# Activations and the scaled input 48 bytes lower, and more products read in four passes, in a bidirectional encoder layer

## The chip, the cores and the metric

The kernel runs on one core of a Trainium2 chip. The metric is the device time of one execution in microseconds. Before the change the median of three runs is 835.85 us (835.64 to 836.09).

The core has a matrix engine (TensorE, with a separate instruction that loads the weights, "PEld" in the profile), VectorE (DVE), ScalarE (ACT), GpSimd (POOL) and SyncE (SP), which issues most transfers. A matrix product names a stationary operand of 128x128 ("weights") and a moving operand of 128 rows and up to 512 columns. Both lie in the on-chip memory, which has 128 partitions; an address in this document is a byte offset within a partition.

## The reference

The layer has a half-step feed-forward block, a mixer (Fourier groups beside attention), a second half-step block, and a last norm, on 512 positions of 1024 channels:

```
x = x + 1/2 * SwiGLU_1(RMSNorm(x))
h = RMSNorm(x); u = h @ w_in                 # [fourier 512 | q 512 | k 128 | v 128]
x = x + concat([A, B]) @ w_out               # A: Fourier mixer, B: attention
x = x + 1/2 * SwiGLU_2(RMSNorm(x))
y = RMSNorm_final(x)
def swiglu(h, w_gate, w_up, w_down):
    return (jax.nn.silu(h @ w_gate) * (h @ w_up)) @ w_down
```

The inner width of the feed-forward block is 2752, that is 21 chunks of 128 and a tail of 64. All is float32.

## The kernel before

**Split numbers.** Every float32 operand of a large product is split into a high and a low part, each in a rounded format that TensorE takes (`fp32r`). A product of weights W and moving operand M is then three matrix products that add up in one PSUM bank: W high with M high, W high with M low, W low with M high. The helper `product` issues them (lines 181, 183 and 184). ScalarE makes the high parts (a cast), VectorE the low ones (a subtraction, `lows`, line 123).

**Straight and turned.** `product` has an option `turn` (lines 176 to 180; the matrix product itself stands on line 179). `turned` (line 172) views 512 columns as 32 blocks of four granules of four numbers, and goes over the first granule of every block, then over the second of every block, and so on: four passes, each in pieces of 16 bytes that lie 64 bytes apart. Both the moving operand and the PSUM output are walked in that order, so that each number lands where it did before. Down products of the full 512 positions are turned; all others are read straight through.

**Feed-forward block (`ffn`, line 277).** The chunks are in four groups. In the first group (3 or 4 chunks with the tail, "plain"), gate and up are computed directly from the scaled input h: `gate` (line 303) loads the weights of one chunk, splits them into two slots, and issues 8 x 3 products of 128x512. In the very first opening (`opening1`, line 680) the first four column chunks are computed together while x arrives, by the matrix product on line 703. The other chunks take seven half-size products instead of eight (`seven`, with products of 128x256 on line 415, moving operand `rt`). After each group the down products of this group are issued for eight blocks of output channels (`down`, line 480; the tail's products are on lines 497 and 498), and the result is added to x (line 538).

**Mixer.** The projections to q, k and v (`project_ops`, line 812) use `product` with h as the moving operand. The Fourier projection has h as the stationary operand and the weights as the moving one (lines 1008 to 1010). Everything in the mixer stands in an order written out by hand (`ORDER`), for all engines; in the feed-forward blocks TensorE and SyncE follow program order and a planner places the rest.

**Closing.** In the last block the final three channel blocks are computed with 128x256 products for the first half of the positions and then by position, with the activations as weights and the down weights as the moving operand (line 529, 128x384).

**Where things lie.** `ring` is one tile with 12 slots of 4096 bytes. Its first eight slots hold h, high part in the first half of a slot and low part in the second (`hh`, `hl`); later the same slots hold weights. Slots 8 to 11 are always weight slots; slots 10 and 11 lie a further 256 bytes up (`ROOM`). `at` holds the activations in seven places of 4096 bytes (2048 of high and 2048 of low part); while the first group runs, the last four places are lent as weight slots. In the mixer `more` gives two more slots. `room` puts unused bytes between tiles. By the allocation of the built program, `ring` begins at byte 16512, `at` at 119232, `rt` at 148032 and `more` at 119168; modulo 256 that is 128, 192, 64 and 128. `FURTHER` (in numbers of four bytes) moves the Fourier weights up within a slot, `SKIP` the down weights of the last three blocks.

Of the kernel before, what the change touches and what calls it, by code (L numbers as in the profile page):

```python
# [7 lines left out]
F32R = mybir.dt.float32r  # L8
# [5 lines left out]
P = 128  # L14
S = 512
D = 1024
KD = D // P
# [4 lines left out]
HD = 64  # L22
EPS = 1e-6
WARM = 9
FURTHER = 48
FURTHER_IN = "f0", "f1", "f2", "f3"
ROOM = 64
NS = 12

GROUPS1 = ((0, "t", 1, 2), range(3, 9), range(9, 15), range(15, 21))  # L30
# [3 lines left out]
USES = "a11", "a12", "s1", "s2", "s4", "s3", "a22"  # L34
PIECES = (0, 2, 2, 0, 2, 1, 1)
KH = KD // 2
SKIP = 32
LAST = 3
CUT = 1, P // 2
HI_DVE = ("f0", "f1")  # L40
# [43 lines left out]
def encoder(ctx, tc, A, out):  # L84
# [1 line left out]
    cp = ctx.enter_context(tc.tile_pool(name="const", bufs=1))  # L86
    wp = ctx.enter_context(tc.tile_pool(name="weights", bufs=3))

    ring = cp.tile([P, NS * KD * P + 2 * ROOM], F32R, name="ring")
    taken = []  # L90

    def room(pool, n):
# [15 lines left out]
    gains = gx[:, : 4 * KD].rearrange("p (n k) -> p n k", k=KD)  # L108
    xt = gx[:, 4 * KD :].rearrange("p (k s) -> p k s", s=S)
    x = [xt[:, k, :] for k in range(KD)]  # L110
    hh = [ring[:, k * KD * P : k * KD * P + S] for k in range(KD)]
    hl = [ring[:, k * KD * P + S : (k + 1) * KD * P] for k in range(KD)]


    def in_order():
# [161 lines left out]
    def ffn(norm, after, wgu, wd, wdt, groups, opening, closing):  # L277
# [4 lines left out]
        n_ = norm.n  # L282
        n_plain = len(groups[0])
        with tc.tile_pool(name=f"act{n_}", bufs=1) as ap, tc.tile_pool(name=f"sums{n_}", bufs=2) as sp:
            room(ap, 256)
            at = ap.tile([P, PLACES, 2, S], F32R, name=f"at{n_}")
            room(ap, 128)
            rt = ap.tile([P, 7, 2, KH, HALF], F32R, name=f"rt{n_}")
            wt, raws = [], {}
            free, where = list(range(PLACES)), {}  # L290
# [12 lines left out]
            def gate(c, between={}, by_dma=False):  # L303
                whi, wlo = weights(wgu[c], f"gu{n_}_{c}", by_dma=by_dma)
                ps = bank(f"gu{n_}_{c}")
                for k in range(KD):
                    between.get(k, int)()
                    product(ps, whi[:, k, :], wlo[:, k, :], hh[k], hl[k], k == 0, k == KD - 1)
                return ps

            def tail_weights():
# [231 lines left out]
            for gi, group in enumerate(groups):  # L543
                last = gi == len(groups) - 1
                ahead = []
                if gi:
                    rest = seven(range(group[0] + 1, min(group[-1] + 2, NF)), ready)
                else:
                    lent = [at[:, i].rearrange("p a b -> p (a b)") for i in range(PLACES - 4, PLACES)]
                    plain.extend(lent)  # L550
                    row = []
                    pss = dict(enumerate(opening(gate, lambda: norm.column([norm.acc]), lambda: row.append(norm.row()))))
                    back(lent[:2])
                    due, parts, left = [*pss, "t"], list(range(KH)), range(2 * len(pss), 2 * n_plain)
                    pss["t"] = [gate(2 * NF)]
                    tail_weights()
                    for i, c in enumerate(left):
                        pss.setdefault(c // 2, []).append(gate(c, by_dma=i in (1,) if n_ else i > 0))
                        if due:
                            j = due.pop(0)  # L560
                            evacuate(at[:, place(j)], n_, pss[j], norm)
                        if c % 2 and c != left[-1]:
                            due.append(c // 2)
                        while len(parts) * len(left) > (len(left) - 1 - i) * KH:
                            o = parts.pop(0)
                            operands(row[0], o, o + 1)

                    def rest():
                        evacuate(at[:, place(n_plain - 1)], n_, pss[n_plain - 1], norm)

                def added(d, ps):
                    residual(d, ps, every)
                    if last:
                        (after.sums if closing else after.add)(d)
                    if ahead:
                        f, *a = ahead.pop(0)
                        f(*a)

                waiting, downs = [], []
                for d in range(KD):  # L580
                    if last and closing and d == KD - LAST:
                        closing(
                            [(e, down(e, group, gi)) for e in range(d, KD)], residual,
                            lambda ps, c: by_tokens(ps, c, group), finished,
                        )
                        break
                    if last and d == KD - 2:
                        back(lent)
                    ps = bank(f"dn{n_}_{d}_{gi}")
                    while len(downs) < min(d + 1 + (0 if gi or not n_ else 2), KD):  # L590
                        downs.append(down(len(downs), group, gi))
                    steps = downs[d](ps, every)
                    for _ in range(len(group) - (last and d < 2)):
                        next(steps)
                    waiting.append((d, ps, steps))
                    if d == (1 if gi or n_ else 2) and not last:
                        ready = prepare(groups[gi + 1][0] + 1)
                        ahead.extend(ready[1])
                    if d == 0:
                        rest()  # L600
                        if last:

                            lent = slots[KD - 2 : KD]
                            plain[2:2] = lent
                            continue
                    for d_, ps, steps in waiting:
                        for _ in steps:
                            pass
                        added(d_, ps)
                    waiting = []  # L610
                for f, *a in ahead:
                    f(*a)
                if not gi:
                    back(lent)
                free.extend(where[j] for j in group)
# [64 lines left out]
    def opening1(gate, column, row):  # L680

        pss = [bank(f"gu0_{c}") for c in range(4)]
        ws = []

        def highs(i, k):
            n0.scale_high(k, None if k else nc.vector)
            hi, _ = ws[i]
            for c in (slice(0, 2), slice(2, 4)) if k == 0 else (slice(0, 4),):
                nc.scalar.copy(hi[:, k % 2, c], raws[i][:, k % 2, c])

        def weight_lows(i, k):
            hi, lo = ws[i]
            lows(lo[:, k % 2], raws[i][:, k % 2], hi[:, k % 2])

        def products(k):
            hi, lo = ws[k // 2]
            passes = [(c, w, m) for w, m in ((hi, hh), (hi, hl), (lo, hh)) for c in range(4)]
            for n, (c, w, m) in enumerate(passes):
                if (k, n) == (6, 8):
                    sums()  # L700
                if (k, n) == (7, 4):
                    row()
                nc.tensor.matmul(  # L703
                    pss[c], w[:, k % 2, c], m[k], start=k == 0 and m is hh and w is hi,
                    stop=k == KD - 1 and w is lo,
                )

        ss = []

        def sums():  # L710
            ss.append(bank("ss0"))
            for c in range(4):
                n0.sum(ss[0], c, [n0.acc])

        with tc.manual_schedule(engines={mybir.EngineType.Activation, mybir.EngineType.DVE}):
            for k in range(KD):
                i = k // 2
                if k % 2 == 0:
                    ws.append(tuple(slot().rearrange("p (a c b) -> p a c b", a=2, b=P) for _ in range(2)))
                highs(i, k)  # L720
                if k < KD - 1:
                    n0.scale_low(k)
                    weight_lows(i, k)
                for j in {3: range(0, 4), 5: (4, 5), 6: (6, 7)}.get(k, ()):
                    n0.sums(j)
            for k in range(KD - 1):
                products(k)
            n0.scale_low(KD - 1)
            n0.mean(ss[0], 0, 4)
            n0.power(0, 4)  # L730
            weight_lows(KH - 1, KD - 1)
            products(KD - 1)
        nc.sync.dma_start(out=qkg, in_=A["qkg"])
        nc.sync.dma_start(out=fb, in_=A["fb"])
        return [pss[0:2], pss[2:4]]
# [6 lines left out]
    with tc.tile_pool(name="mix", bufs=1) as mp, tc.tile_pool(name="mixt", bufs=1) as mt:  # L742
# [69 lines left out]
        def project_ops(c, name):  # L812

            weight_ops(f"w{name}", A["wins"][c])

            def step(k):
                if k == 0:
                    banks[name] = bank_for(name, {"v": 1, "k": 3, "q0": 3}.get(name, 2))
                whi, wlo = ws[f"w{name}"]
                product(banks[name], whi[:, k, :], wlo[:, k, :], hh[k], hl[k], k == 0, k == KD - 1)  # L820

            for k in range(KD):
                op(f"{name}.{k}")(lambda k=k: step(k))
# [737 lines left out]
```

## Time and profile before

| what | time |
|---|---|
| median of three runs | 835.85 us |
| the profiled execution | 835.62 us |
| its span, first to last instruction | 833.8 us |
| TensorE busy in the span | 826.7 us, 5406 products |
| VectorE busy | 640.0 us |
| ScalarE busy | 465.1 us |
| granted TensorE clock, mean | 0.998 |

In the profile a group of instructions has its line, engine, operation, output and inputs, shape and count, then the busy time in us, the mean duration of one in ns, and the idle time just before. The durations of matrix products overlap, since a product starts while the one before it drains; how often a product can start is read from the starts in the timeline. In the timeline and in the chain the first number of a row is its start in us from the span's start, the second its length.

### The profile page before, as it was taken

To read this page: it belongs to the slowest core of one execution; us is meant where nothing else is said; L and a number is where in the kernel's file an instruction comes from. 1 tells how busy PE (TensorE), PEld (TensorE's weight loads), DVE (VectorE), ACT (ScalarE), POOL (GpSimd) and SP (SyncE) were. 2 spreads that over 40 slices of the span, in tenths; PEclk is the share of its full clock that TensorE was granted. 3 is DMA by queue.
4 is the path that set the end of the run, shared out by engine and by line. 5 is a ranking of instruction groups with operands and counts; after the bars stand their busy time and mean duration, and the time that the engine had idled before them with its cause. 6 is when DMAs were issued, how large, how long until landed. Compare 5 with 4: busy or idle time off the path is not lost.

```text
span 833.8 us, 13667 instructions
## 1 busy us (share of the span) xinstructions
PE 826.7 (99%) x5406; PEld 750.9 (90%) x5406; DVE 640.0 (77%) x1005; ACT 465.1 (56%) x778; POOL 30.7 (4%) x34
## 2 busy tenths in 40 slices
PE   9999999999999999999999999999999999999997
PEld 6888999899989998888998888899988999899986
DVE  7898896489756947699998488999955896479573
ACT  7773674157524645677786356656632674257462
POOL 0110000000000000221100000100000000000001
PEclk9999999999999999999999999999999999999999
DMA  7664322323242213522020224453232332322222
GB/s 253 170 144 167 129 93 77 121 102 139 74 141 98 65 55 114 177 94 79 26 76 26 73 88 130 109 170 121 89 116 88 133 116 66 135 102 95 68 75 102
DMA packets 31168, 89.58 MB, mean 107 GB/s; under 512 B 3712, under 2 KB 8832, under 8 KB 31104
## 3 DMA queue, kind: packets, MB, share of 16 engines
q1 hardware_dynamic: 27776, 82.61, 28.8%
q0 software_dynamic: 2608, 5.12, 3.3%
q10 hardware_dynamic: 720, 0.98, 0.3%
q8 instruction: 42, 0.69, 0.3%
q14 instruction: 22, 0.18, 0.1%
HBM read 84.24 MB, written 2.10 MB: 104 GB/s over the span
## 4 chain that ended last, share of the span: by engine, by line
PE 98%; issue 0%; DMA 0%; DVE 0%; ACT 0%; POOLq 0%; POOL 0%; DVEq 0%
PE dn L179 25%; PE r L415 23%; PE q L415 11%; PE p L415 6%; PE mix L181 3%; PE mix L184 3%; PE mix L183 3%; PE gu L703 3%; PE gu L181 3%; PE gu L183 3%; PE gu L184 3%; PE mix L1213 2%; PE mix L1170 2%; PE mix L1144 1%; PE mix L1008 1%; PE mix L1009 1%
## 5 line engine op out<-in xcount | busy, mean ns | idle before, releaser
L415 PE MATMUL r<-rt,ring 128*128 128x256 f32 x1686 | 209.5, 276 | 0.0
L179 PE MATMUL dn<-at,ring 128*128 128x512 f32 x900 | 205.4, 383 | 0.0
L415 PEld LDWEIGHTS r<-rt,ring 128*128 128x128 f32 x1686 | 200.5, 188 | 0.9
L179 PEld LDWEIGHTS dn<-at,ring 128*128 128x128 f32 x900 | 167.7, 187 | 31.5
L415 PE MATMUL q<-rt,ring 128*128 128x256 f32 x840 | 106.6, 276 | 0.0
L123 DVE TENSOR_TENSOR ring<-s,ring 128x1024 fp32r<-128x1024 f32 x70 | 85.4, 1220 | 24.1 <-ACT ring L374 20.8
L415 PEld LDWEIGHTS q<-rt,ring 128*128 128x128 f32 x840 | 100.4, 188 | 0.0
L538 DVE SCALAR_TENSOR_TENSOR gx<-dn,gx 128x512 f32<-128x512 f32 x61 | 41.9, 688 | 71.4 <-PE dn L179 71.3
L374 ACT CAST ring<-s 128x1024 fp32r<-128x1024 f32 x70 | 73.5, 1050 | 28.0 <-PE p L415 12.7
L165 ACT CAST ring<-raw_dn 128x768 fp32r<-128x768 f32 (+3 forms) x58 | 45.3, 784 | 75.4 <-PE dn L179 66.9
L123 DVE TENSOR_TENSOR ring<-raw_dn,ring 128x768 fp32r<-128x768 f32 (+3 forms) x58 | 51.5, 891 | 5.8 <-PE r L415 4.5
L415 PE MATMUL p<-rt,ring 128*128 128x256 f32 x420 | 53.3, 276 | 0.0
L123 DVE TENSOR_TENSOR ring<-raw_g,ring 128x1024 fp32r<-128x1024 f32 x35 | 42.6, 1218 | 10.3 <-PE p L415 10.3
L415 PEld LDWEIGHTS p<-rt,ring 128*128 128x128 f32 x420 | 50.2, 188 | 0.0
L374 ACT CAST ring<-raw_g 128x1024 fp32r<-128x1024 f32 x35 | 36.8, 1052 | 14.6 <-DMA raw_g<-in_wgu 8.8
L423 ACT COPY p<-r 128x256 f32<-128x256 f32 x35 | 13.0, 370 | 47.9 <-PE r L415 47.6
L447 ACT ACTIVATE g<-g 128x512 f32<-128x512 f32 x35 | 22.2, 633 | 23.4 <-DVE g L446 23.1
L383 ACT CAST ring<-raw_u 128x512 fp32r<-128x512 f32 x35 | 21.8, 624 | 16.5 <-PE q L415 15.9
L460 DVE TENSOR_TENSOR u<-g,u 128x512 f32<-128x512 f32 x35 | 24.0, 685 | 6.4 <-ACT u L459 6.4
L251 POOL TENSOR_TENSOR r<-ms,mhalf 128x4 f32<-128x4 f32 (+1 forms) x4 | 4.3, 1072 | 665.7 <-DVE ms L244 665.7
L181 PE MATMUL gu<-ring 128*128 128x512 f32 x72 | 28.2, 392 | 0.0
L123 DVE TENSOR_TENSOR at<-u,at 128x512 fp32r<-128x512 f32 x35 | 23.9, 684 | 5.5 <-ACT at L461 5.5
(310 smaller groups left out, 1471.0 us busy)
## 6 DMA issues: line engine op xcount, KB each, us to landing
raw_g<-in_wgu SPq DMA_DIRECT2D x35, 512.0 KB, 3.6
raw_u<-in_wgu SPq DMA_DIRECT2D x35, 512.0 KB, 4.3
raw_dn<-in_wd SPq DMA_DIRECT2D x40, 384.0 KB, 3.1
raw_gu<-in_wgu SPq DMA_DIRECT2D x12, 512.0 KB, 3.8
raw_o<-in_wo SPq DMA_DIRECT2D x8, 512.0 KB, 3.5
raw_dn<-in_wd SPq DMA_DIRECT2D x8, 448.0 KB, 3.3
raw_wq<-in_wins SPq DMA_DIRECT2D x4, 512.0 KB, 4.5
raw_f<-in_winf SPq DMA_DIRECT2D x4, 512.0 KB, 4.1
```

Of the source, the lines that this page charges most:

```text
L123: nc.vector.tensor_tensor(out=lo, in0=src, in1=asf(hi), op=ALU.subtract)
L165: nc.scalar.copy(hi[:, :n, :], raw[:, :n, :])
L179: nc.tensor.matmul(ps, a, b, start=first and b is mhi and a is whi, stop=last and a is wlo)
L181: nc.tensor.matmul(ps, whi, mhi, start=first, stop=False)
L183: nc.tensor.matmul(ps[:, t], whi, mlo[:, t], start=False, stop=False)
L184: nc.tensor.matmul(ps, wlo, mhi, start=False, stop=last)
L374: nc.scalar.copy(hi, src)
L415: nc.tensor.matmul(ps[:, t], a[:, ks], b[:, i, t], start=first and i == 0 and o == 0, stop=i == KH - 1 and o == 2, skip_group_check=not first,
L447: nc.scalar.activation(b["g"], b["g"], AF.Silu)
L460: nc.vector.tensor_tensor(out=u, in0=b["g"], in1=u, op=ALU.mult)
L538: nc.vector.scalar_tensor_tensor(out=x[d][:, t], in0=ps[:, t], scalar=0.5, in1=x[d][:, t], op0=ALU.mult, op1=ALU.add)
L703: nc.tensor.matmul(pss[c], w[:, k % 2, c], m[k], start=k == 0 and m is hh and w is hi, stop=k == KD - 1 and w is lo,)
```

## The change

The change alters where three things lie and how they are read; the operations and their order on each engine stay the same.

- The ring's tile begins with 16 numbers in front (`FRONT`), and the slots come after them, so that the slots and every tile allocated behind the ring lie 64 bytes higher. h starts 4 numbers from the tile's start (`NEAR`), which is 48 bytes below its slots and 16 bytes above where it was.
- The activations' tile gets 64 numbers more, in place of the 256 bytes of room before it, and the places start 16 - 12 = 4 numbers from its start (`LOWER`). The lent places stay 16 numbers from the start. The built program has the places at 119184, 48 bytes below 119232, and the lent ones at their old addresses; modulo 256 the ring's slots, `more`, the tail weights and the lent places are now at 192, h and the places at 144, `rt` at 128.
- `FURTHER` and `SKIP` become smaller by 12 and 28 numbers.
- Plain gate and up products, those of `opening1`, and the mixer's projections are turned.

A slot now reaches 48 bytes into the part of h that follows, and a lent place 48 bytes into the next place.

```diff
-FURTHER = 48
+FURTHER = 36
...
+FRONT, LOWER, NEAR = 16, -12, 4
...
-SKIP = 32
+SKIP = 4
...
-    ring = cp.tile([P, NS * KD * P + 2 * ROOM], F32R, name="ring")
+    whole = cp.tile([P, FRONT + NS * KD * P + 2 * ROOM], F32R, name="ring")
+    ring = whole[:, FRONT:]
...
-    hh = [ring[:, k * KD * P : k * KD * P + S] for k in range(KD)]
-    hl = [ring[:, k * KD * P + S : (k + 1) * KD * P] for k in range(KD)]
+    hh, hl = (
+        [whole[:, k * KD * P + o * S + NEAR : k * KD * P + (o + 1) * S + NEAR] for k in range(KD)] for o in range(2)
+    )
...
-            room(ap, 256)
-            at = ap.tile([P, PLACES, 2, S], F32R, name=f"at{n_}")
             room(ap, 128)
+            acts = ap.tile([P, PLACES * 2 * S + ROOM], F32R, name=f"at{n_}")
+            at = acts[:, FRONT + LOWER : FRONT + LOWER + PLACES * 2 * S].rearrange("p (n a b) -> p n a b", a=2, b=S)
...
-                    product(ps, whi[:, k, :], wlo[:, k, :], hh[k], hl[k], k == 0, k == KD - 1)
+                    product(ps, whi[:, k, :], wlo[:, k, :], hh[k], hl[k], k == 0, k == KD - 1, turn=True)
...
-                    lent = [at[:, i].rearrange("p a b -> p (a b)") for i in range(PLACES - 4, PLACES)]
+                    lent = [acts[:, FRONT + i * KD * P : FRONT + (i + 1) * KD * P] for i in range(PLACES - 4, PLACES)]
...
-                    pss[c], w[:, k % 2, c], m[k], start=k == 0 and m is hh and w is hi,
+                    turned(pss[c]), w[:, k % 2, c], turned(m[k]), start=k == 0 and m is hh and w is hi,
...
-                product(banks[name], whi[:, k, :], wlo[:, k, :], hh[k], hl[k], k == 0, k == KD - 1)
+                product(banks[name], whi[:, k, :], wlo[:, k, :], hh[k], hl[k], k == 0, k == KD - 1, turn=True)
```

## The prediction

> **What bounds the kernel now.** I read the page's totals first, then the chain that ended last, then the groups by form, and last the timeline, because only the distance from one start to the next tells what a matrix product costs here.
>
> ```profile
> span 833.8 us, 13667 instructions
> ...
> PE 826.7 (99%) x5406; PEld 750.9 (90%) x5406; DVE 640.0 (77%) x1005; ACT 465.1 (56%) x778; POOL 30.7 (4%) x34
> ...
> PE 98%; issue 0%; DMA 0%; DVE 0%; ACT 0%; POOLq 0%; POOL 0%; DVEq 0%
> PE dn L179 25%; PE r L415 23%; PE q L415 11%; PE p L415 6%; PE mix L181 3%; PE mix L184 3%; PE mix L183 3%; PE gu L703 3%; PE gu L181 3%; PE gu L183 3%; PE gu L184 3%; PE mix L1213 2%; PE mix L1170 2%; PE mix L1144 1%; PE mix L1008 1%; PE mix L1009 1%
> ```
>
> TensorE is the whole chain. Next, the groups that the change touches (count behind the x; lines 183 and 184 have a row like each of line 181, line 498 one like line 497), and one it leaves alone:
>
> ```profile
> L415 PE MATMUL r<-rt,ring 128*128 128x256 f32 x1674 | 209.3, 276 | 0.0
> L179 PE MATMUL dn<-at,ring 128*128 128x512 f32 x900 | 205.4, 383 | 0.0
> ...
> L181 PE MATMUL gu<-ring 128*128 128x512 f32 x72 | 28.2, 392 | 0.0
> ...
> L181 PE MATMUL mix<-ring 128*128 128x512 f32 x32 | 12.8, 400 | 0.0
> ...
> L179 PE MATMUL dn<-at 128*128 128x512 f32 x45 | 12.1, 387 | 0.0
> L703 PE MATMUL gu<-ring,at 128*128 128x512 f32 x48 | 11.9, 399 | 0.0
> L703 PE MATMUL gu<-ring 128*128 128x512 f32 x48 | 11.2, 392 | 0.3 <-ACT ring L689 0.3
> L181 PE MATMUL gu<-ring,at 128*128 128x512 f32 x24 | 9.5, 396 | 0.0
> ...
> L529 PE MATMUL last<-ring,at 128*128 128x384 f32 x42 | 8.5, 345 | 0.0
> ...
> L181 PE MATMUL mix<-ring,more 128*128 128x512 f32 x16 | 6.5, 408 | 0.0
> ...
> L497 PE MATMUL dn<-at,wt 128*128 128x512 f32 x16 | 6.2, 385 | 0.0
> ```
>
> They hardly wait (last column). Their durations overlap the next product, so the price is the distance of starts. From the timeline, plain gate products and mixer projections, all read straight through:
>
> ```profile
> 34.23 0.39 PE L181 MATMUL gu<-ring 128*128 128x512 f32 x1
> ...
> 39.67 0.40 PE L181 MATMUL gu<-ring,at 128*128 128x512 f32 x1
> ...
> 45.27 0.39 PE L181 MATMUL gu<-ring 128*128 128x512 f32 x1
> ```
>
> ```profile
> 336.02 0.39 PE L181 MATMUL mix<-ring 128*128 128x512 f32 x1
> ...
> 341.46 0.39 PE L181 MATMUL mix<-ring 128*128 128x512 f32 x1
> ```
>
> 24 products lie between each two rows: 5.44 us / 24 = 226.7 ns with weights in the ring, 5.60 / 24 = 233.3 ns with weights in a lent place of `at`, and 5.44 / 24 = 226.7 ns in the mixer. Down products already read in 4 passes; from the chain, and from the timeline of the first group:
>
> ```profile
> 137.39 28.13 PE dn L179 x126
> ```
>
> ```profile
> 59.34 0.38 PE L497 MATMUL dn<-at,wt 128*128 128x512 f32 x1
> 59.55 0.38 PE L498 MATMUL dn<-at,wt 128*128 128x512 f32 x1
> 59.77 2.14 PE L179 MATMUL dn<-at,ring 128*128 128x512 f32 x9
> 61.76 0.38 PE L497 MATMUL dn<-at,wt 128*128 128x512 f32 x1
> 61.98 0.38 PE L498 MATMUL dn<-at,wt 128*128 128x512 f32 x1
> 62.20 1.49 PE L179 MATMUL dn<-at,ring 128*128 128x512 f32 x6
> ...
> 72.09 1.52 PE L179 MATMUL dn<-at 128*128 128x512 f32 x6
> 73.45 0.83 PE L179 MATMUL dn<-at,ring 128*128 128x512 f32 x3
> ```
>
> 28.13 / 126 = 223.3 ns is the usual price. From 59.34 to 62.20 13 products take 2.86 us: 220.0 ns. From 72.09 to 73.45 6 products with weights in lent places take 226.7 ns. So the same shape costs 220 to 233 ns by pass order and by where the operands lie.
>
> **What the addresses do.** Call d the distance from the moving operand to the weights that are loaded during it, in bytes of a partition modulo 256. By the tiles' places before, d is 0 for gate and projections with weights in ring or `more`, 64 for gate weights in lent places, 192 for down with ring or tail weights, 0 for down with lent weights, 64 for the 128x256 products of line 415. So: straight through, d=0 gives 226.7 and d=64 gives 233.3; in 4 passes, d=192 gives 223.3 or 220.0 and d=0 gives 226.7. After the change ring, `more`, tail weights and lent places agree modulo 256 and h and the activations lie below them, so that d is 48 for every gate, up, projection and down product, lent or not. Those of line 415, and the 128x256 ones that `FURTHER` and `SKIP` are for, keep d=64, so their time stays. No row has d=48, nor any 128x512 read in 4 passes from a start that is not a multiple of 64 bytes: X, the price of a 4-pass product at d=48, is the unknown.
>
> **The change part by part.** On every engine the sequence of operations stays the same; no wait, DMA or instruction is added. X is bounded from below by a step as large as that between the two 4-pass prices under the lower one (220.0 - 3.3 = 216.7, an estimate, since no mean in the rows is less), and from above by the dearest place seen, 233.3. I take 220.0: it is the price that today's 4-pass products hold for a stretch, and d is now one value throughout, so nothing knocks them from it as the lent weights after 63 us do. No row proves this.
>
> The Trainium skill, "TensorE: Matmul & The Clock Gate", section "Step-by-step: what each phase is for", says that the weight load and the moving operand have read ports of their own, so the next load takes nothing from the running product. Then place would not matter, X would be today's 223.3, and the first rival below would come true; the 226.7 against 233.3 above, where only the weights' place differs, disagrees.
>
> With X = 220.0:
> - Gate and up, ring weights: 3 x 72 + 48 = 264 products x 6.7 = 1.77 us.
> - Gate and up, lent weights: 3 x 24 + 48 = 120 x 13.3 = 1.60 us, since these also leave d=64.
> - Projections: 3 x (32 + 16) = 144 x 6.7 = 0.96 us.
> - Down, ring weights: 900 x 3.3 = 2.97 us; lent: 45 x 6.7 = 0.30; tail: 2 x 16 = 32 x 3.3 = 0.11.
>
> Sum 7.7 us, all on the chain. Taken back:
>
> ```profile
> 28.70:56.20 27.50, 27.50 (x123) 22.59 (x122) 26.55 (x48) 21.97 (x31) 5.44 (x5) 1.00 0.75 159
> 536.40:551.00 14.60, 14.60 (x68) 12.11 (x66) 14.54 (x25) 6.51 (x11) 0.00 (x0) 1.00 0.50 164
> ```
>
> ```profile
> 24.42 2.11 PE L703 MATMUL gu<-ring,at 128*128 128x512 f32 x8
> 26.42 0.65 PE L256 MATMUL rp<-ident,r 128*128 128x128 f32 x4
> ```
>
> ```profile
> 24.84 1.53 POOL L251 TENSOR_TENSOR r<-ms,mhalf 128x4 f32<-128x4 f32 x1 [23.53 <-DVE ms L244]
> ```
>
> (Windows: stretch, its length, busy time of PE, weight loads, DVE, ACT, POOL.) In 28.70 to 56.20 TensorE would save 96 x 6.7 + 24 x 13.3 = 0.96 us, which leaves 26.54 against VectorE's 26.55: the cover is used up, and part of VectorE's idle time is its own waiting, so I take off 0.3. In 536.40 to 551.00 VectorE is busy for 14.54 of 14.60; of some 64 products' 0.37 us saved (14.45 / 64 = 225.8 each now) I count 0.3 as lost to its results coming no earlier. The norm's power ends at 24.84 + 1.53 = 26.37, the transposes start at 26.42: the 8 products between run 0.1 us shorter and wait for it. The closing's 42 products of 128x384 take their weights from `at` and move the ring, so they go from d=64 to d=208; by the step from 226.7 to 233.3 up to 42 x 6.7 = 0.28 us either way, and I take 0.2 lost. A ring slot now reaches 48 bytes into the next part of h, and a lent place 48 bytes into the next place; these new conflicts are between uses a whole stage apart: nothing, and if a cast had to wait, one 128x1024 cast's time, about 1 us. Writes by ACT and DVE at the new starts: nothing, as both are off the chain; a dearer write would show in the two windows above.
>
> In all 7.7 - 0.9 = 6.8 us off. The profiled execution took 835.62 us (span 833.8 and 1.8 around it), 0.23 under the median of 835.85: 835.62 - 6.8 = 828.8 us.
>
> **Rivals.**
> *The place does not matter (X = 223.3).* Order of passes alone counts. Gains 264 x 3.4 + 120 x 10.0 + 144 x 3.4 + 45 x 3.4 = 2.7 us, less 0.2 of cover: 833.1. For it: 126 products in a row at just this price. Against: 220.0 and 226.7 at other places.
> *A better place than any seen (X = 216.7).* 264 x 10.0 + 120 x 16.7 + 144 x 10.0 + 900 x 6.6 + 45 x 10.0 + 32 x 6.6 = 12.7 us, less about 1.4 of cover: 824.3. For it: 16-byte offsets were never tried in the rows, and 64-byte steps move the price by 6.7. Against: nothing has been that fast.
> *The weight load now collides with the passes (X = 226.7), slower.* d=48 lies between 0 and 64, and 4 passes at d=0 already cost 226.7. Lent gate products still gain 120 x 6.7 = 0.8, but down loses 900 x 3.4 + 32 x 3.4 = 3.2, and the closing 0.2: 838.2. It decides from X = 224.8 on, where the gate's gains and the down's losses cancel. At the worst place, 233.3, ring gate and projections lose 408 x 6.7 = 2.7, down 900 x 10.0 + 45 x 6.7 + 32 x 10.0 = 9.6: 848. For it: those 6 products; against: the run at 220 shows the 4-pass order can do better, and one place in four is all that speaks for loss.
>
> The Trainium skill, "Advanced Engine Details and Errata", section "PSUM Cachelines", says that any non-contiguous PSUM access slows matmuls markedly; gate and projections now write PSUM in 16-byte pieces. By it these 528 would lose; the 900 down products write so already, at 223.3 against 226.7, and disagree, so it has no more than 0.02 of the slower chance.
>
> **How the numbers follow.** X near 220: 0.33; near 223.3: 0.20; near or under 216.7: 0.22; 225 and more: 0.25. The predicted time is the first's, 828.8, its own range 826 to 831.5. The range, 821.5 to 839.5, takes in the three other cases and leaves out X under 215 and over 227.5. A change within 0.2% (1.7 us), about what a measurement of this kernel can tell from none, needs X between 223.7 and 225.9: 0.06. Faster: 0.33 + 0.22 + most of 0.20 = 0.71; slower 0.23.
>
> **What would show it.** Right: 126 down products of a group in 27.7 us instead of 28.13; 24 gate products in 5.28 us whether from ring or lent places; 24 projections likewise; 12 of the 128x256 products still 1.36 us apart. Wrong: down above 28.3 us per 126, or TensorE standing before the first 128x256 products of the stages at 76 or 551 us with VectorE as releaser, which would mean that VectorE and not the price of a product bounds those stages.

## The result and the profile after

| | before | after |
|---|---|---|
| median in this comparison | 835.76 us (4 runs) | 829.39 us (828.99 to 829.76, 4 runs) |
| the profiled execution | 835.62 us | 829.21 us |
| its span | 833.8 us | 827.4 us |
| TensorE busy | 826.7 us | 820.0 us |

The ratio after to before is 0.9923, with an interval of 0.9906 to 0.994. In the profiled executions 6.4 us of span went, where 6.8 were forecast. The ratios below, each with its 95% interval, compare all undisturbed executions of two kernels in one comparison, so they need not be the quotient of the two medians.

The changed kernel's lines are three higher from the matrix product on: line 182 is the turned product (179 before), 418 the half-width one (415), 500 and 501 the tail's (497 and 498), 706 that of the opening (703), 126 VectorE's subtraction (123). The page's totals and the groups by form of the changed kernel:

```profile
span 827.4 us, 13668 instructions
PE 820.0 (99%) x5406; PEld 750.9 (91%) x5406; DVE 639.4 (77%) x1005; ACT 464.6 (56%) x778; POOL 30.7 (4%) x34
```

```profile
L418 PE MATMUL r<-rt,ring 128*128 128x256 f32 x1674 | 209.0, 276 | 0.0
L182 PE MATMUL dn<-at,ring 128*128 128x512 f32 x900 | 203.3, 380 | 0.4 <-DVE ring L126 0.4
...
L182 PE MATMUL gu<-ring 128*128 128x512 f32 x216 | 48.9, 381 | 0.0
...
L182 PE MATMUL gu<-ring,at 128*128 128x512 f32 x72 | 16.3, 380 | 0.0
```

The mean durations barely moved (383 to 380 ns for down): they overlap and say nothing of the price. One thing is new in the last column, VectorE as releaser of a down product. The price is in the starts. From the timeline of the changed kernel, gate products with weights in the ring, then in lent places, then in the ring; and two stretches of half-width products:

```profile
32.83 5.66 PE L182 MATMUL gu<-ring 128*128 128x512 f32 x25
38.33 5.44 PE L182 MATMUL gu<-ring,at 128*128 128x512 f32 x24
43.61 2.58 PE L182 MATMUL gu<-ring 128*128 128x512 f32 x11
...
77.74 1.52 PE L418 MATMUL r<-rt,ring 128*128 128x256 f32 x12
79.10 1.07 PE L418 MATMUL q<-rt,ring 128*128 128x256 f32 x8
```

5.50 us / 25 = 220.0 ns and 5.28 / 24 = 220.0 ns: ring and lent places now cost the same. The half-width products stay at 1.36 / 12 = 113.3 ns. From the chain of waits, a whole group of down products:

```profile
134.91 27.72 PE dn L182 x126
```

27.72 / 126 = 220.0 ns, where it was 223.3. From the timeline, the first projections:

```profile
330.83 8.08 PE L182 MATMUL mix<-ring 128*128 128x512 f32 x36
338.75 0.95 PE L240 MATMUL mix<-ones,acc 128*128 128x2 f32 x8
```

7.92 / 36 = 220.0 ns as well. I added up the distances of starts over all of TensorE's products in both traces. What each kind gained or lost, in us:

| products | forecast | measured |
|---|---|---|
| gate and up, 384 | -3.37 | -3.18 |
| down, 977 | -3.38 | -2.12 (of which waits +1.13) |
| projections, 144 | -0.96 | -1.1 |
| closing, 42 of 128x384 | +0.2 | +0.05 |
| half-width products on `rt` | 0 | -0.3 |
| rest of the mixer | 0 | +0.4 |
| start, until the first weights are there | 0 | -0.2 |

The forecast also put 0.7 us on waits of TensorE: 0.3 in each of two stretches and 0.1 at the norm.

The +1.13 stands in one place, the first group of the second feed-forward block. The wait that the profile lists, then TensorE's and VectorE's timeline there:

```profile
PE dn L182 <- DVE ring L126: 0.4, 1, 0.4
```

```profile
535.13 1.28 PE L182 MATMUL dn<-at,ring 128*128 128x512 f32 x5
536.83 0.49 PE L182 MATMUL dn<-at,ring 128*128 128x512 f32 x1 [0.42 <-DVE ring L126]
```

```profile
535.15 0.69 DVE L126 TENSOR_TENSOR ring<-raw_u,ring 128x512 fp32r<-128x512 f32 x1
535.75 0.68 DVE L541 SCALAR_TENSOR_TENSOR gx<-dn,gx 128x512 f32<-128x512 f32 x1
536.36 0.42 DVE L126 TENSOR_TENSOR ring<-raw_dn,ring 128x256 fp32r<-128x256 f32 x1
```

The low part of the down weights of block 3 is made from 536.36 on, behind the next chunk's low part and the addition of block 0. The last of the five products stands for it: 819 ns from its start to the next instead of 220. Four more waits of 0.11 to 0.20 us follow until 542.6. Before the change this group ran without such a wait:

```profile
541.19 1.50 PE L179 MATMUL dn<-at,ring 128*128 128x512 f32 x6
541.34 0.41 DVE L123 TENSOR_TENSOR ring<-raw_dn,ring 128x256 fp32r<-128x256 f32 x1
```

There the low part of block 3 was ready at 541.75 us, and its product, the last of the six, started at 542.31. After the change it is ready 5.0 us earlier, but TensorE comes 6.1 us earlier.

### The profile page after: what moved, and what is told of

The parts are those of the page before. It is cut to its first block, busy times and chain, and to the rows that moved or that the text cites. A ratio compares the mean times of both kernels' runs of the same rounds, so it can differ in the third digit from the quotient of the medians.

```text
span 827.4 us, 13668 instructions
## 1 busy us (share of the span) xinstructions
PE 820.0 (99%) x5406; PEld 750.9 (91%) x5406; DVE 639.4 (77%) x1005; ACT 464.6 (56%) x778; POOL 30.7 (4%) x34
## 4 chain that ended last, share of the span: by engine, by line
PE 97%; issue 1%; DVE 1%; DMA 0%; ACT 0%; POOLq 0%; POOL 0%; DVEq 0%
PE dn L182 25%; PE r L418 23%; PE q L418 12%; PE gu L182 8%; PE p L418 6%; PE mix L182 4%; PE gu L706 3%; PE mix L187 2%; PE mix L186 2%; PE mix L184 2%; PE mix L1216 2%; PE mix L1173 2%; PE mix L1147 1%; PE mix L1013 1%; PE mix L1148 1%; PE mix L1011 1%
## 5 line engine op out<-in xcount | busy, mean ns | idle before, releaser
L182 PE MATMUL dn<-at,ring 128*128 128x512 f32 x900 | 203.3, 380 | 0.4 <-DVE ring L126 0.4
L182 PE MATMUL gu<-ring 128*128 128x512 f32 x216 | 48.9, 381 | 0.0
L182 PEld LDWEIGHTS gu<-ring 128*128 128x128 f32 x216 | 40.4, 188 | 6.9
```

The source lines that it names most:

```text
L182: nc.tensor.matmul(ps, a, b, start=first and b is mhi and a is whi, stop=last and a is wlo)
```

## The experiments

The price of a product is its distance from start to start, and d is how far the weights that are loaded during it lie above its moving operand, in bytes modulo 256, as in the prediction.

### Each half of the change alone

The first kernel is the kernel before with the new pass order only:

```diff
-                    product(ps, whi[:, k, :], wlo[:, k, :], hh[k], hl[k], k == 0, k == KD - 1)
+                    product(ps, whi[:, k, :], wlo[:, k, :], hh[k], hl[k], k == 0, k == KD - 1, turn=True)
...
-                    pss[c], w[:, k % 2, c], m[k], start=k == 0 and m is hh and w is hi,
+                    turned(pss[c]), w[:, k % 2, c], turned(m[k]), start=k == 0 and m is hh and w is hi,
```

> Places as before, but plain gate and up products, those of the opening and the projections read in 4 passes (d=0 with ring weights, d=64 with lent ones). Theory 'place': it is d=48 that makes 220 ns, the order alone does not; then 24 gate products with ring weights stay near 24 x 226.7 = 5.44 us, as the few 4-pass products at d=0 did, 126 down products stay at 28.13 us, and the time stays within 1.5 us of 835.8. Rival 'order': 4 passes cost 223.3 ns wherever the operands lie; then 24 gate products take 5.36 us with ring and with lent weights, and the time is about 833.

The second is the changed kernel with these lines and that of the projections put back (straight), at the new places:

> Places as in the changed kernel, but gate, up and projections read straight through as before. Theory 'place': 126 down products take 27.72 us (220.0 ns each), which is 3.3 us off; straight products at d=48 should lie between the 226.7 of d=0 and the 233.3 of d=64, so they gain nothing or lose up to 2 us: 832.5 to 834.5. Rival 'order': down stays at 28.13 us per 126, time 835.8 less what the lent gate weights gain, about 835.

Order alone: 836.57 us, ratio 0.9995 (0.998 to 1.0009). Places alone: 834.87 us, ratio 0.9985 (0.9974 to 0.9995), a little above its forecast. In this comparison and the next one the kernel before has a median of 836.06 us. Timeline and chain of order alone, gate products with d = 0 (ring) and 64 (lent):

```profile
29.71 9.90 PE L179 MATMUL gu<-ring 128*128 128x512 f32 x43
39.46 5.59 PE L179 MATMUL gu<-ring,at 128*128 128x512 f32 x24
44.89 5.32 PE L179 MATMUL gu<-ring 128*128 128x512 f32 x23
```

```profile
136.92 28.13 PE dn L179 x126
```

9.75 / 43 = 226.7 ns and 5.43 / 24 = 226.3 ns. In four passes a ring product costs here what it cost straight, 226.7; summed over all, the 264 ring products gain 0.44 us (228.7 to 227.0 ns in the mean) and the 120 lent ones 0.77 (233.3 before, in the stretch). Timeline and chain of places alone, where gate products are straight at d = 48 and down products turned at d = 48; eight times three products lie between the two rows:

```profile
30.07 0.39 PE L184 MATMUL gu<-ring 128*128 128x512 f32 x1
...
35.59 0.39 PE L184 MATMUL gu<-ring 128*128 128x512 f32 x1
```

```profile
137.73 27.72 PE dn L182 x126
```

Straight, the new place is dearer, 5.52 / 24 = 230.0 ns here and 235.5 in the mean over the second block's gate products (230.7 there before); down products are at 220.0, all of their gain. Summed over starts against the kernel before:

| | gate and up | down | all 512-wide products of the mixer |
|---|---|---|---|
| order alone | -1.22 | +0.53 | -0.27 |
| places alone | +1.38 | -3.00 | +1.01 |
| both | -3.18 | -2.12 | -0.90 |

So neither part gains much by itself, and for gate products they do not add up: -1.22 and +1.38 alone, -3.18 together. Down products, turned in every kernel, gain by the place alone.

### Other distances, the same everywhere

The prediction took 220.0 because one distance would hold everywhere. Here it does, at another distance: all 512-wide products that are turned at d = 192, or all at d = 32.

```diff
-FURTHER = 36
+FURTHER = 0
...
-FRONT, LOWER, NEAR = 16, -12, 4
+FRONT, LOWER, NEAR = 64, -48, 16
...
-SKIP = 4
+SKIP = 32
```

(and 192 bytes of room before and behind the activations, one `ROOM` less in the ring.)

> All products of the changed kernel in 4 passes, but at d=192 throughout, the distance that most down products had before. The prediction's reason for 220 was that one distance throughout lets the products settle at the price that was seen for a stretch; theory 'one distance' then gives 220.0 ns here too, 27.72 us per 126 down products, 829.4. Theory 'this distance': d=192 costs 223.3 as before, 28.13 us per 126, and the time is 829.4 + 1500 x 3.3 ns = about 834 less the VectorE waits that go, 833 to 834.

```diff
-FURTHER = 36
+FURTHER = 40
...
-FRONT, LOWER, NEAR = 16, -12, 4
+FRONT, LOWER, NEAR = 16, -8, 8
...
-SKIP = 4
+SKIP = 8
```

> The changed kernel with d=32 throughout (h and activations 32 bytes below their slots instead of 48). 'One distance': 220.0 ns, 829.4. 'This distance': any other price between 217 and 233; between d=0 (226.7) and d=48 (220.0) the middle would be 223, 833.

At 192 the median is 833.67 us, the ratio 0.9976 (0.9958 to 0.9994); at 32 the median is 839.43 us, the ratio 1.0039 (1.0021 to 1.0057). Timeline and chain at d = 192:

```profile
29.66 9.54 PE L182 MATMUL gu<-ring 128*128 128x512 f32 x42
39.04 5.52 PE L182 MATMUL gu<-ring,at 128*128 128x512 f32 x24
```

```profile
136.25 28.13 PE dn L182 x126
```

and at d = 32:

```profile
29.79 9.68 PE L182 MATMUL gu<-ring 128*128 128x512 f32 x42
39.31 5.61 PE L182 MATMUL gu<-ring,at 128*128 128x512 f32 x24
```

```profile
137.07 28.54 PE dn L182 x126
```

At 192: 9.38 / 42 = 223.3 ns for gate products, 28.13 / 126 = 223.3 for down. At 32: 9.52 / 42 = 226.7 and 28.54 / 126 = 226.5, not the 223 guessed for the middle. One distance throughout does not bring 220.0; this distance does. Sixteen bytes lie between a kernel that is 0.8% faster and one that is 0.4% slower.

### Distances beside each other, one for h and one for the activations

The next three kernels give h and the activations distances of their own (the lent places move up by 256 bytes). The edit of the first; the second has -44 and 2, the third -60 and 0 in place of -28 and 12, and `FURTHER` and `SKIP` follow so that the Fourier products and the closing's half-width ones keep their distances:

```diff
-FRONT, LOWER, NEAR = 16, -12, 4
+FRONT, LOWER, NEAR, LENT = 16, -28, 12, 80
...
-            acts = ap.tile([P, PLACES * 2 * S + ROOM], F32R, name=f"at{n_}")
-            at = acts[:, FRONT + LOWER : FRONT + LOWER + PLACES * 2 * S].rearrange("p (n a b) -> p n a b", a=2, b=S)
+            acts = ap.tile([P, PLACES * 2 * S + 2 * ROOM], F32R, name=f"at{n_}")
+            at = acts[:, LENT + LOWER : LENT + LOWER + PLACES * 2 * S].rearrange("p (n a b) -> p n a b", a=2, b=S)
```

> Two distances in one kernel: d=16 for gate, up and projections, d=112 for the down products. 112 is 48 + 64, and its start within 64 bytes is that of d=48. Theory 'within 64 bytes': only the start within 64 bytes counts, so 126 down products take 27.72 us (220.0 each). Theory 'within 256 bytes': d counts as a whole, and down costs something else, 222 to 230 ns, 28.0 to 29.0 us. Gate at d=16: no forecast better than the 226.6 of d=0 and the 226.7 of d=32.

> d=56 for gate, up and projections, so that each piece of four numbers begins 8 bytes into a 16-byte granule and lies across two; d=176 (48 + 128) for down. Theory 'granule': a piece across two granules costs two reads, gate over 230 ns each, 24 over 5.52 us; otherwise about 220 to 226. Down: 'within 64 bytes' 27.72 us per 126, 'within 256 bytes' something else.

> d=64 for gate, up and projections, d=240 (48 + 192) for down. Gate: the lent gate products of the run with the order alone stood at d=64 at a mean of 226.5 ns, so 24 in 5.44 us. Down: 'within 64 bytes' 27.72 us per 126; 'within 256 bytes' something else.

Each was executed once: 839.19, 961.35 and 852.3 us. The chain's down groups at d = 112, 176 and 240, one kernel each, and the timeline of the second's gate products at d = 56:

```profile
139.62 28.00 PE dn L182 x126
```

```profile
186.27 28.96 PE dn L182 x126
```

```profile
50.44 21.80 PE L182 MATMUL gu<-ring 128*128 128x512 f32 x48
72.03 8.30 PE L182 MATMUL gu<-ring,at 128*128 128x512 f32 x18
```

```profile
141.71 28.71 PE dn L182 x126
```

That is 222.2, 229.8 and 227.9 ns for down. Within a 64-byte block the places 112, 176 and 240 are the same as 48, which costs 220.0: the place in 64 bytes does not decide, the one within 256 does. Whether that is the distance or the moving operand's own address is not settled by these kernels, since their weights all lie at 192 modulo 256 and only the moving operand was shifted. For the distance speaks that the weights' address alone changes the price (turned, with the moving operand at 192 in the kernel before: 223.3 with weights at 128, 226.7 with weights at 192), and that d = 0 costs 226.7 with both at 128 (gate products, order alone) and with both at 192 (down products with lent weights, before). At d = 56 a piece of 16 bytes starts in the middle of a 16-byte granule, and a gate product costs 21.59 / 48 = 449.8 ns, twice the price. The Trainium skill, "SBUF — State Buffer", section "Specifications (TRN2)", gives that memory 16-byte cachelines and says that each cross to a new line pays; it states no size, and this row agrees with it. The price holds at half speed too: in two windows of this kernel, 42.87 to 46.20 and 592.50 to 595.70 us, the granted clock was 0.50, and the products still started 446 to 464 ns apart, so there it was not TensorE's clock that set it.

All the prices of a 128x512 product, from stretches as above (means over the gate products where a range stood):

| d | 0 | 16 | 32 | 48 | 56 | 64 | 112 | 176 | 192 | 240 |
|---|---|---|---|---|---|---|---|---|---|---|
| four passes, ns | 226.7 | 231 | 226.5 | 220.0 | 450 | 226 to 232 | 222.2 | 229.8 | 223.3 | 227.9 |
| straight, ns | 226.7 | | | 230 to 236 | | 233.3 | | | | |

The sums of two of these kernels are not made by these prices alone. In the first and third of them the half-width products on line 418 also got dearer, by 4.0 and 10.3 us over all starts against the kernel before, although their d is still 64; in the third a stretch of the timeline reads

```profile
83.75 1.58 PE L418 MATMUL q<-rt,ring 128*128 128x256 f32 x12
85.17 2.99 PE L418 MATMUL r<-rt,ring 128*128 128x256 f32 x24
```

1.42 / 12 = 118.3 ns instead of 113.3. In the second, with `rt` at the same place, they cost 113.6 in the mean. The price goes by whole groups: in the first kernel one group of each block stands at 118 and the others at 113, in the third all but one at 118, with operands at the same places in every group. So here one distance has two prices, and what chooses between them stays open; with one execution each it is also open whether this belongs to the kernels or to these executions. The down products of each of these kernels cost the same in every full group.

### The waits in the second block

The first attempt takes the low parts of the down weights of blocks 3, 5 and 6 off VectorE: ScalarE writes the high part with its sign turned into the low part's place, and a transfer adds the weights to it.

```diff
-                whi, wlo = weights(src, "", len(js), raw, skip=SKIP if halves_ else 0)
+                whi, wlo = weights(src, "", len(js), raw, skip=SKIP if halves_ else 0, by_dma=n_ == 2 and gi == 0 and d in (3, 5, 6))
```

> The changed kernel, but in the first group of the second feed-forward block the low parts of the down weights of blocks 3, 5 and 6 are made by ScalarE and an accumulating transfer in place of VectorE's subtraction. Theory 'VectorE is the bound there': the 64 down products of this stage lose the waits of 0.60, 0.11, 0.11, 0.20 and 0.12 us (1.1 us together over 220 ns each) or most of them, and the stage from its first down product to the first product of 128x256 takes 14.1 to 14.4 us in place of 15.2; time 828.3 to 828.9. Rival 'something else is late': the wait stays where it is, with another releaser, and the time stays at 829.4.

835.57 us, ratio 0.9994 (0.9981 to 1.0006): the whole gain of the change is gone, where 828.3 to 828.9 was forecast. Waits, GpSimd's issues and TensorE's timeline of this kernel:

```profile
PE dn L182 <- DMA ring<-in_wd: 4.8, 3, 2.1
```

```profile
534.59 0.88 POOL L156 DMA_DIRECT2D ring<-in_wd  x1 [11.00 <-DVE s L392]
537.42 0.86 POOL L156 DMA_DIRECT2D ring<-in_wd  x1 [1.94 <-ACT ring L155]
540.30 0.85 POOL L156 DMA_DIRECT2D ring<-in_wd  x1 [2.02 <-ACT ring L155]
```

```profile
547.34 0.80 PE L182 MATMUL dn<-at,ring 128*128 128x512 f32 x1 [2.10 <-DMA ring<-in_wd]
547.93 0.63 PE L500 MATMUL dn<-at,wt 128*128 128x512 f32 x1
548.36 0.63 PE L501 MATMUL dn<-at,wt 128*128 128x512 f32 x1
```

The second and third adding transfers wait for ScalarE's part, and the three products wait 1.3 to 2.3 us for the transfers. After that the products start 427 ns apart until 550.5 us: TensorE ran at half speed, and the granted clock was 0.50 from 548 to 550 us. The Trainium skill, "TensorE: Matmul & The Clock Gate", section "What's actually happening", says that the clock is halved after an idle window of about 3.4 us; none of the waits was that long, so here busy stretches between waits did not keep it: in the 3.41 us before 547.29 TensorE was busy for 1.36 us. The remedy was worse than the wait, and told nothing of VectorE's queue.

The second attempt starts the next chunk one block later:

```diff
-                    if d == (1 if gi or n_ else 2) and not last:
+                    if d == (1 if gi else 2) and not last:
```

> The changed kernel, with the preparation of the next chunk in the first group of the second feed-forward block issued one block of down products later, so that low parts of down weights stand ahead of it in VectorE's queue. Theory, the 1.1 us of waits between 536.0 and 542.6 us come from low parts that stand behind other VectorE work: they shrink, 828.3 to 829.2 us, and no long gap comes elsewhere. Rival, VectorE's total work bounds this stretch, whatever its order: the waits move to the 128x256 products behind 551 us, 829.4 us or more.

829.47 us (ratio 0.9926, 0.9911 to 0.9941), with the same wait as before it:

```profile
537.14 0.49 PE L182 MATMUL dn<-at,ring 128*128 128x512 f32 x1 [0.40 <-DVE ring L126]
```

By the traces the order of work on every engine is that of the changed kernel all the same, so neither theory was tried. It is a second measurement of the changed kernel, 0.1 us away from the first.

The third takes time out of VectorE's queue, without a change of what is waited for; in that group the kernel leaves out most columns of the addition to x:

```diff
-                    residual(d, ps, every)
+                    residual(d, ps, slice(0, 64) if n_ == 2 and gi == 0 else every)
```

> The changed kernel, but in the first group of the second feed-forward block the eight residual additions on VectorE take 64 of the 512 columns (the other columns are left out of the sum), so that each takes some 0.1 to 0.2 us of VectorE instead of 0.69, and nothing else is changed. Theory, the waits of 0.60, 0.11, 0.11, 0.20 and 0.12 us between 536.0 and 542.6 us come from low parts of down weights that stand behind other VectorE work: the first shrinks to about 0.1, the others go, and the 85 products from 536.4 end about 1 us earlier; 828.2 to 828.8 us. Rival, the weights of these blocks arrive late from memory or from ScalarE's cast: the waits stay within 0.1 us of what they were, 829.2 to 829.7 us.

829.14 us (ratio 0.9916, 0.9895 to 0.9937). VectorE's and then TensorE's timeline:

```profile
535.80 0.22 DVE L541 SCALAR_TENSOR_TENSOR gx<-dn,gx 128x64 f32<-128x64 f32 x1
535.94 0.41 DVE L126 TENSOR_TENSOR ring<-raw_dn,ring 128x256 fp32r<-128x256 f32 x1
...
538.81 1.21 DVE L126 TENSOR_TENSOR ring<-s,ring 128x1024 fp32r<-128x1024 f32 x1
539.94 0.75 DVE L126 TENSOR_TENSOR ring<-raw_dn,ring 128x256 fp32r<-128x256 f32 x2
```

```profile
539.60 0.62 PE L182 MATMUL dn<-at,ring 128*128 128x512 f32 x2
540.41 0.49 PE L182 MATMUL dn<-at,ring 128*128 128x512 f32 x1 [0.19 <-DVE ring L126]
```

The low part of block 3 starts at 535.94 instead of 536.36, and the wait for it shrinks from 0.60 to 0.14 us (362 ns between starts). That is VectorE's queue and not a late arrival. But all the waits together fell only from 1.13 to 0.74 us: the planner now put a subtraction of 1.21 us ahead of the low part of block 5, which costs 0.37 us at 540. The forecast for this run, about 1 us, was too large for that reason. The time alone shows no gain, since its interval overlaps that of the change; the wait in the trace does.

### Further products at the good distance

The half-width products, over half of TensorE's products, got the same treatment: `rt` 16 bytes higher, so that d = 48, and four passes.

```diff
-            rt = ap.tile([P, 7, 2, KH, HALF], F32R, name=f"rt{n_}")
+            rts = ap.tile([P, 14 * KH * HALF + FRONT], F32R, name=f"rt{n_}")
+            rt = rts[:, RT : RT + 14 * KH * HALF].rearrange("p (n a k s) -> p n a k s", a=2, k=KH, s=HALF)
...
-                                    ps[:, t], a[:, ks], b[:, i, t], start=first and i == 0 and o == 0,
+                                    turned(ps[:, t]), a[:, ks], turned(b[:, i, t]), start=first and i == 0 and o == 0,
```

> The changed kernel, with the 128x256 products (2934 of them, moving operand rt) also read in four passes, and rt 16 bytes higher, so that d is 48 for them as well. Theory, the price belongs to the four passes at this distance and not to the width: they start 110.0 ns apart instead of 113.3, which is 2934 x 3.3 = 9.8 us at most; VectorE and the arrival of low parts hold some of it back as they did 1.1 us in the second block, so 820 to 824 us. Rival one, the price belongs to the 512-wide walk (32 blocks in a pass): the half products, with 16 blocks in a pass, stay at 113.3 or get dearer, 829 us or more. Rival two, other engines set the pace in the groups of seven products: 110.0 between neighbours, but new waits with VectorE or ScalarE as releaser, and a gain under 3 us.

834.01 us (ratio 0.9976, 0.9966 to 0.9986), some 4.6 us worse than the change. From the timeline:

```profile
81.56 1.54 PE L420 MATMUL q<-rt,ring 128*128 128x256 f32 x12
82.94 2.91 PE L420 MATMUL r<-rt,ring 128*128 128x256 f32 x24
```

1.38 / 12 = 115.0 ns, in the mean over all 114.7: 3.8 us more than in the changed kernel, where up to 9.8 less were expected. (The profiled execution took 835.77 us; some 2 us of that is a slower start, see the last section.) Single starts lie 109, 115, 117 and 118 ns apart, and I found no address of the operand, the weights or the bank that sorts them. Rival one came true in its effect; why a pass of 16 blocks does not do what one of 32 does stays open.

The output projection's 192 products are 512 wide. Their operands, the mixer's results, were put into one tile 48 bytes under the weights, and turned:

```diff
-        room(mp, 32)
+        blend = mp.tile([P, 16 * S + 4], F32R, name="blend")
+        room(mp, 32)
+        lines = [blend[:, 4 + i * S : 4 + (i + 1) * S] for i in range(16)]
...
-                product(banks[name], whi[:, k, :], wlo[:, k, :], *m, k == 0, k == KD - 1)
+                product(banks[name], whi[:, k, :], wlo[:, k, :], *m, k == 0, k == KD - 1, turn=True)
```

(`qa`, `qb`, `eh` and `el` are these lines instead of tiles of their own.)

> The changed kernel, with the output projection's 192 products of 128x512 also in four passes, and their moving operands in one tile whose lines lie 48 bytes below the weights modulo 256 (the queries' weights for the scores move with them, to a distance of 208 from the keys). Theory, the price follows the four passes at this distance, whatever tile the operand is in: 220.0 instead of 226.7, 192 x 6.7 = 1.28 us; the 40 score products at 208 may cost up to 6.7 more or less, 0.3 either way; so 827.8 to 828.6 us. Rival, the price at 48 is a property of the pair ring and h or of the activations, and not of the distance: the products stay at 226 to 227, 829.2 us or more.

828.28 us (828.15 to 828.68), ratio 0.9899 (0.9882 to 0.9916): the best kernel here, its executions all under those of the change (828.99 to 829.76). The intervals of the two ratios overlap, so its lead rests on the executions and the trace:

```profile
469.97 8.08 PE L182 MATMUL mix<-blend,ring 128*128 128x512 f32 x36
477.89 0.82 PE L182 MATMUL mix<-blend,more 128*128 128x512 f32 x3
```

7.92 / 36 = 220.0 ns, in yet another tile, with weights in the ring as in `more`. Of 192 x 6.7 = 1.28 us the wait for the low part of block 3 takes 0.26 (1084 ns from start to start instead of 819), which leaves 1.02; counted from the first real product (at 5.47 us of a span of 826.9, and at 4.93 of 827.4) to the end of the span, 1.07 went.

## Why the prediction was right, and where not

**The price.** X = 220.0 was taken and 220.0 came, for gate, up, down, projections and lent weights alike; the terms of the sum follow from it (-3.37, -3.38 and -0.96 against -3.18, -3.25 without waits and -1.1). The first rival, the order of passes alone, falls with the first experiment: in four passes at the old places ring products stayed near 227, not at 223.3. The second and third, 216.7 and 226.7, were about the same unknown; the third came true at the neighbouring place, where d = 32 gives 226.5 and a kernel slower by 0.4%, and nothing came near the second. No row of before could have told 48 from 32.

**Its reason.** "d is now one value throughout, so nothing knocks them from it" is wrong. At d = 192 throughout, down products stay at 223.3. The 220.0 that stood for a stretch at 59 us of the kernel before was at most a hint of what the shape can do; it was the right number for a wrong reason, and so in part luck: the prediction itself gave a price near 220 a chance of 0.33.

**Straight against turned.** The prediction priced only turned products at d = 48, as it had to. It did not see that straight ones get dearer there (230 to 236, where the kernel before had 226.7 with ring weights), so that the two parts of the change need each other.

**The two rules.** By the Trainium skill's "TensorE: Matmul & The Clock Gate", section "Step-by-step: what each phase is for", the weight load reads through a port of its own. Then the distance between weights and moving operand could not matter; but with the moving operand at one address the weights' address alone gave 223.3 or 226.7, and the places tried gave 220.0 to 231 in four passes. The rule of the Trainium skill's "Advanced Engine Details and Errata", section "PSUM Cachelines", on non-contiguous writes would have made the turned gate products dearer; they write 16-byte pieces at 220.0, less than straight ones at 226.7, and so do the output projection's products in the last experiment.

**VectorE's cover.** Here the sum was off. In 28.70 to 56.20 I took 0.3 off and nothing was lost: from 26.83 on the gate products took 29.35 us before and 28.25 after, as priced. In 536.40 to 551.00 I took 0.3 off and 1.13 was lost. VectorE's busy share of the window had warned of it, but I priced only results that come no earlier, and not the order: the low part of block 3 stands behind an addition and another chunk's low part, and with 1.3 us of gate time saved ahead of it TensorE comes earlier than its turn. The thin addition shows it: 0.42 us out of the queue took 0.46 off that wait. So the mis-sized term of the sum is this one, 0.3 for a measured 1.13.

**The small terms.** The power chain's 0.1 is seen as 360 ns from one start to the next at 25.16 us, some 0.14 over the price; before the change that step was 291 ns. The closing's 42 products cost 0.05 instead of 0.2. The new overlaps of ring slots and lent places caused no wait of TensorE.

**What would have shown it wrong** was half there: VectorE as releaser, in the block at 536 us rather than before the half-width products. The stage's own 64 products had 0.37 us to gain; with 1.13 us of waits it became longer, 15.27 us from its first down product to the first half-width one, where it was 14.45.

## What to carry to other kernels

Price matrix products by the distance of their starts in the timeline, and sort them by where their operands lie before touching anything else: here 16 bytes decided between 220.0 and 226.5 ns, and the pass order and the place had to be right together. When a stage gets faster, look at what stands ahead of each small piece of preparation in the helper engine's queue, not at its busy share alone. Don't carry a good setting over to another shape without a run: it worked for the output projection and cost 3.8 us for the half-width products.

## What the runs showed of the hardware that was not expected

- The price of a 512-wide product in four passes of 16-byte pieces changes with the place of the weights loaded meanwhile and of the moving operand within 256 bytes, with no simple pattern: 226.7, 231, 226.5, 220.0 at a distance of 0, 16, 32 and 48, and 222.2, 229.8, 223.3, 227.9 at 112, 176, 192 and 240. Why is open.
- Pieces that straddle a 16-byte granule double the price (450 ns, one kernel), at full and at half clock alike.
- Three waits of 1.3 to 2.3 us within 12 us brought TensorE to half speed (427 ns) for some 3 us. No wait is needed for it: in the kernel with d = 56 TensorE counts as busy for the whole 3.41 us from 39.45 to 42.86 us, with products 453 ns apart and eight tiny ones, and the granted clock was 0.50 from 42.87 to 46.20.
- At the very start two kernels ran their first nine or so products at 427 ns, until 9.4 and 9.7 us, which cost about 2 us. There TensorE had waited 0.66 and 0.53 us for the first weights; with 0.15, 0.44 and 0.52 us in others, but also with 0.7 us in the last kernel, it had not slowed. It looks like chance of some 2 us: no edit of these kernels was meant to touch it.
